# RWKV recurrence: one operand for state and outputs by tokens, head norm by tokens, inverse in two threads, exact overlaps and new prices in the emitter

## The chip, the cores and the metric

The kernel runs on one core of a Trainium2 chip. The metric is the device time of one execution in microseconds, lower is better. One core has five engines with a queue each: PE (matmuls), DVE and POOL (elementwise work), ACT (functions and copies) and SP, which here issues nearly all DMAs. Each engine works through its instructions in the order in which the program gives them.

## The reference, cut to what matters

One layer of a streaming encoder on 512 prompt tokens and 32 sample tokens: a joint input projection, three recurrent branches (SSD, GLA, RWKV-7), gates, output projection, cross attention. The change is in the RWKV branch:

```
S_new = S * w_t - (S @ kk_t) (kk_t * a_t)^T + v_t k_t^T        # per token, 16 heads of 64 x 64
o_t   = S_new @ r_t
o_rwkv = (head_layernorm(o7, ln_w, ln_b) + bonus) * silu(rgate)
```

The kernel computes it in chunks of 64 tokens: eight chunks for the prompt and one, number 8, for the sample. In a chunk the delta rule needs the inverse of a 64x64 triangular matrix per head.

## The kernel before, in words

A Python emitter writes out the whole program once (class `Sched`). It keeps a clock for each engine and a price for each operation, and runs generator threads in order of priority: a thread yields the time at which its next operand will be ready, and in the meantime the next thread emits. Prices decide only the order of the instructions; the chip then runs that order, with semaphores. The thread of lowest priority, `dense()`, emits the projections: 48 matmuls `pd` (272 columns, type f32r) for each block of weights, each block loaded (`wraw`), split by ACT into `wh` and by DVE into `wl`.

Of the blocks, 16 of 24 matmuls (memory keys and values), 2 and 24 (r, k, v) feed phase 1, the RWKV branch. 48 further blocks are fill (gates), emitted where nothing else is ready; the last 8 of them are held until late in phase 2 (`HOLD2`). So 384 + 26 x 48 + 40 x 48 = 3,552 dense matmuls can be emitted before phase 2 (SSD and GLA, `P2a`) opens, which `main()` does when all RWKV threads are done; phase 2 brings 28 blocks of its own.

RWKV runs by pairs of heads p = 0 to 7, in four threads: `rw_A` (decays, the products PP, tokens TK), `rw_I` (the inverse: 31 small steps on POOL, then matmuls pW, pT), `rw_C` (the recurrence over chunks 8, 0 to 7) and `rw_N` (head norm, bonus, store of y). A chunk of `rw_C` is a chain: matmul of the state (`pc<-Sn,AR`), DVE sum R, matmul `pc<-R,TT`, DVE predicated copy, matmul for the new state (`pc<-TK`), DVE update Sn. The outputs come from `pc<-AR,Sd` and `pc<-PP,TK`. Chunk 0 has no state, so it lacks the first and one of the others. `Sched.mm` prices an f32 matmul with a weight of more than 64 columns at 210 ns or more; f32 matmuls run as two passes, each with a weight load (PEld). `rw_N` sums over heads with f32r matmuls against a block matrix (`pl`, `pv`).

Of the kernel before, what the change touches and what calls it, by code (L numbers as in the profile page):

```python
# [8 lines left out]
F32 = mybir.dt.float32  # L9
# [93 lines left out]
class Pool:  # L103
# [5 lines left out]
    def tile(self, shape, dtype, name, tag=None, bufs=None):  # L109
        ring = self.rings.setdefault(tag or name, [])  # L110
        n = bufs or self.bufs
        if len(ring) >= n:
            self.S.flush(ring[-n])
        t = self.pool.tile(shape, dtype, name=name, tag=tag or name, **(dict(bufs=bufs) if bufs else {}))
        if len(ring) >= n:
            last = {}
            for v in self.S.reg.get(ring[-n], {}).values():
                for x in v:
                    for e, u in x.items():
                        last[e] = max(last.get(e, 0.0), u)  # L120
            self.S.reg[t.name] = {(0, 1 << 30, 0, 128): ({}, last)}
        ring.append(t.name)
        return t


class Sched:
# [57 lines left out]
    def span(self, a):  # L184
        x = a.ap
        if a.space == DRAM:
            return (a.offset, a.offset + sum((n - 1) * abs(s) for s, n in x) + 1, 0, 1)
# [4 lines left out]
        return (lo, lo + sum((n - 1) * s for s, n in x[1:]) + 1, p0, p0 + x[0][1])  # L192

    def since(self, a, which, e="pe"):
# [4 lines left out]
        lo, hi, p0, p1 = self.span(a)  # L199
        return max((t + (HOP.get((x, e), 0.0) if x != e or not which else 0.0) for k, v in d.items() if k[0] < hi and lo < k[1] and k[2] < p1 and p0 < k[3]  # L200
# [25 lines left out]
    def mm(self, out, lhsT, rhs, start, stop, transpose=False, shared=False):  # L226
# [102 lines left out]
def body(tc, I, O):  # L329
# [19 lines left out]
    with tc.manual_schedule(), \  # L349
# [242 lines left out]

        def start_mem():
# [36 lines left out]
            sq = slot[0]["TK"].rearrange("p a c h t -> p (a c h t)")[:, :8 * ML].rearrange("p (a t) -> p a t", t=ML)  # L630
# [12 lines left out]
        def start_x():  # L643
            xt = []
            for q, (b, a_) in enumerate(((slot[0]["AR"], 0), (slot[0]["PP"], 0), (slot[0]["PP"], 1), (slot[1]["AR"], 0))):
                yield has(f"load wk{q + W['XL']}")
                b = b if len(b.shape) == 4 else b.rearrange("p c h a t -> p c (h a) t")
                b = b.rearrange("p c a t -> p (c a t)")[:, a_ * 2 * T:(a_ + 1) * 2 * T].rearrange("p (a t) -> p a t", t=T)
# [8 lines left out]
            sq = slot[1]["TK"].rearrange("p a c h t -> p (a c h t)")[:, :T]  # L657
# [190 lines left out]
        def rw_A(p):  # L848
# [87 lines left out]

# [10 lines left out]
            S.tt(ar[:, :, 2, :], ch(rs), EE[:, :, 1:65], MUL)  # L947
            yield S.free("v")
# [15 lines left out]
            tk = d["TK"]  # L964

            def tokens(n_, src):
# [17 lines left out]
            pp = d["PP"]  # L984
            yield S.at(bk, ar)
            for c0, cn in ((0, 4), (4, 4), (8, 1)):
# [3 lines left out]
                for c in range(cn):  # L990
                    for i in range(2):
                        hs = slice(64 * i, 64 * i + 64)
                        S.mm(ps[i][:, c * 128:c * 128 + 128], bk[hs, c0 + c, i:i + 2, :].rearrange("p a t -> p (a t)"),
                             ar[hs, c0 + c, i:3:2 - i], True, True)
                for i in range(2):
                    S.tt(pp[:, c0:c0 + cn, i].rearrange("p c a t -> p c (a t)"), ps[i][:, :cn * 128].rearrange("p (c x) -> p c x", c=cn),
                         C("m_rw").unsqueeze(1).to_broadcast([128, cn, 128]), MUL)
                yield S.free("v")
            for i in range(2):
                S.store(out=rows64(n_scr[p % 2], i), in_=pp[i * 64:i * 64 + 64, :, i, 0, :])  # L1000
# [16 lines left out]
            for n_, (src) in enumerate((vs, kae, bee)):  # L1017
                S.mm(ps[0:64, n_ * 128:n_ * 128 + 128], src[:, 512:576], C("ident"), True, True, transpose=True)
            t8 = rwr.tile([64, 3, 128], F32, name="t8", tag="t8")
            yield S.since(t8, 1) - S.t["pe"]  # L1020
            S.act(t8.rearrange("p c t -> p (c t)"), ps[0:64, :384], AF.Copy)
            for i in range(2):
                h = 64 * i
                S.store(out=tk[64 - h:128 - h, :, 8, i, :], in_=t8[:, 0:2, h:h + 64])
                S.store(out=tk[h:h + 64, 1, 8, i, :], in_=t8[:, 2, h:h + 64])
            done.add(f"rwA{p}")

        def rw_I(p):

# [13 lines left out]
            S.dma(out=td, in_=I["eye3"])  # L1043
            yield has(f"rwN{p}")
            d = slot[p % NSLOT]
            pp, tt_ = d["PP"], d["TT"]
            yield S.stored(pp)
            for g in range(3):
                S.dma(out=nd[g * NB:g * NB + NB], in_=blocks(n_scr[p % 2]))
            yield S.at(nd, td)  # L1050
# [10 lines left out]
            yield S.stored(td)  # L1061
            for h in range(2):
                S.dma(out=tt_[h * 64:h * 64 + 64, :, h * 64:h * 64 + 64], in_=rows64(d_scr, h))
            yield S.at(tt_)
            x1 = rwr.tile([128, 8, 32], F32, name="x1", tag="itmp")
# [29 lines left out]
        def rw_C(p):  # L1095
# [6 lines left out]
            AR, PP, TK, TTt, GC = (d[n_] for n_ in ("AR", "PP", "TK", "TT", "GC"))  # L1102
            VU, KB = TK[:, 0], TK[:, 1]
            st_ = None
            yield S.stored(TK)
            yield S.at(s0r, PP, TK, TTt)
            RV = rwp.tile([128, 9, 64], F32, name="RV", tag="RV")
            for c0, cn in ((4, 5), (0, 4)):
                ps = yield from bank("pr")
                for c in range(cn):  # L1110
                    for i in range(2):
                        hs, gs = slice(64 * i, 64 * i + 64), slice(64 - 64 * i, 128 - 64 * i)
                        S.mm(ps[hs, c * 64:c * 64 + 64], PP[gs, c0 + c, i, 0, :], VU[gs, c0 + c, i, :], True, True)
                S.act(RV[:, c0:c0 + cn].rearrange("p c t -> p (c t)"), ps[:, :cn * 64], AF.Copy)
            for c in [8] + list(range(8)):
# [5 lines left out]
                pu, pS, po = pa[:, 128:256], pa[:, 256:384], pb[:, 0:128]  # L1121
                if Ss is None:
                    R = RV[:, 0]
                else:
                    S.mm(pa[:, 0:64], AR[:, c, 0:2, :].rearrange("p a t -> p (a t)"), Ss, True, True)
                    R = rwp.tile([128, 64], F32, name="R", tag="R", bufs=2)
                    S.tt(R, pa[:, 0:64], RV[:, c], ADD)
# [4 lines left out]
                nc.vector.copy_predicated(VU[:, c], two(C("blk1").bitcast(I32)), two(pu))  # L1132
                S.note("v", 203, (VU[:, c],), (pu,))
                yield max(S.at(VU[:, c]), 0.0 if Ss is None else S.at(Sd))
                S.mm(pS, KB[:, c].rearrange("p a t -> p (a t)"), VU[:, c], True, True)
                if Ss is not None:
                    S.mm(po, Sd.rearrange("p a t -> p (a t)"), both(AR[:, c, 2, :]), True, False)
                S.mm(po, VU[:, c].rearrange("p a t -> p (a t)"), PP[:, c, :, 1, :], Ss is None, True)
                ns = rwp.tile([128, 64], F32, name="Sn", tag="S", bufs=2)
                for i in range(2):  # L1140
                    hs = slice(64 * i, 64 * i + 64)
                    if Ss is None:
                        S.cp(ns[hs], pS[hs, hs])
                    else:
                        S.stt(ns[hs], Ss[hs], GC[hs, c, :], pS[hs, hs], MUL, ADD)
# [4 lines left out]
                for i in range(2):  # L1150
                    hs = slice(64 * i, 64 * i + 64)
                    S.act(AR[hs, c, 2, :], po[hs, hs], AF.Copy)
            done.add(f"rwC{p}")

        def rw_N(p):
# [3 lines left out]
            d = slot[p % NSLOT]  # L1159
            AR = d["AR"]  # L1160
            o7 = AR[:, :, 2, :]
            HC = ((0, 4, 0), (4, 4, 256), (8, 1, 512))

            def rows(t, c, n, o):
                w = min(64 * n, T - o)
                return t[:, o:o + w].rearrange("p (c t) -> p c t", c=n), o7[:, c:c + n, :w // n]

            oh = rwr.tile([128, T], F32R, name="oh", tag="hi")
            ol = rwr.tile([128, T], F32R, name="ol", tag="lo")
            cs = rwr.tile([128, T], F32, name="cs", tag="cs")  # L1170
            sq = rwr.tile([128, T], F32, name="sq2", tag="sq2")
            yield S.at(o7)
            for x in HC:
                h_, a_ = rows(oh, *x)
                parts(a_, h_, rows(ol, *x)[0])
            yield S.at(ol)
            for g, (o, w) in enumerate(((0, 256), (256, 288))):
                ps = yield from bank("pl")
                head_sums(ps[:, :w], oh[:, o:o + w], ol[:, o:o + w])
                for x in ((HC[0],), HC[1:])[g]:  # L1180
                    c_, a_ = rows(cs, *x)
                    S.stt(c_, rows(ps, x[0], x[1], 0)[0] if x[0] < 8 else ps[:, 256:288].unsqueeze(1), -1.0 / 64, a_, MUL, ADD)
                S.act(sq[:, o:o + w], cs[:, o:o + w], AF.Square)
            done.add(f"rwO{p}")
            sh = rwr.tile([128, T], F32R, name="sh", tag="hi")
            sl = rwr.tile([128, T], F32R, name="sl", tag="lo")
            parts(sq, sh, sl)
            yield S.at(sl)
            for (o, w) in HV:
                ps = yield from bank("pv")  # L1190
                head_sums(ps[:, :w], sh[:, o:o + w], sl[:, o:o + w])
                S.act(sq[:, o:o + w], ps[:, :w], AF.Ln, scale=1.0 / 64, bias=LNEPSC)
# [878 lines left out]
```

## Time and profile before

| | |
|---|---|
| median of 3 runs | 1308.95 us (1308.35 to 1311.31) |
| profiled execution | 1308.11 us, span 1306.3 us |
| PE busy | 1268.2 us, 97%, 10752 matmul passes |
| PEld (weight loads) busy | 1225.1 us, 94% |
| DVE, ACT, POOL busy | 840.3, 641.2, 368.2 us |
| chain that ended last | PE 61%, of which pd 47% |

Busy shares are averages: PE's records overlap, so that a matmul's price is read from the starts of its neighbours, not from its duration.

### The profile page before, as it was taken

Reading aid. Unit: us, or ns where it says so; the run is one execution under the profiler, and the core shown is the slowest. Engines: PE = TensorE matmul, PEld = TensorE weight load, DVE = VectorE, ACT = ScalarE, POOL = GpSimd, SP = SyncE. Lnnn points to the kernel's source line nnn. Section 1 sums busy time; section 2 is a strip of 40 time slices with the busy share of each in tenths; the row PEclk is TensorE's granted clock in tenths of the full one; section 3 lists DMA queues with packets and bytes.
Section 4 is the critical chain, followed back from the end, with each engine's and each line's share of the span. In section 5 each row is a group of like instructions: output and inputs, shape, how many; then the busy total and the mean of one; then the engine's idle time right before and its main releaser. Section 6 shows DMA issues by size and latency. Waiting matters only on the chain.

```text
span 1306.3 us, 27334 instructions
## 1 busy us (share of the span) xinstructions
PE 1268.2 (97%) x10752; PEld 1225.1 (94%) x10752; DVE 840.3 (64%) x1723; ACT 641.2 (49%) x1230; POOL 368.2 (28%) x724
## 2 busy tenths in 40 slices
PE   8899999999999999999999999998999999999996
PEld 7899989999999998999999999997999999999996
DVE  5747748767686777444455787576666756566543
ACT  5664554665557473553646455353545323544421
POOL 0712837464474736340101323032100000000000
PEclk8999999999999999999999999998999999999998
DMA  8543454453545354542532333243788345540201
GB/s 290 161 145 97 139 140 102 122 145 97 134 123 144 89 142 124 156 135 90 172 115 73 111 103 119 85 117 88 260 325 275 131 134 189 171 154 20 103 18 69
DMA packets 167696, 176.59 MB, mean 135 GB/s; under 512 B 99841, under 2 KB 122465, under 8 KB 167441
## 3 DMA queue, kind: packets, MB, share of 16 engines
q1 hardware_dynamic: 167136, 174.19, 43.7%
q8 instruction: 85, 1.39, 0.5%
q10 hardware_dynamic: 432, 0.67, 0.2%
q14 instruction: 43, 0.34, 0.1%
HBM read 134.01 MB, written 33.16 MB: 128 GB/s over the span
## 4 chain that ended last, share of the span: by engine, by line
PE 61%; DVE 4%; ACT 1%; issue 0%; DMA 0%; DVEq 0%; SPq 0%; ACTq 0%
PE pd L234 47%; PE pc L234 3%; PE pO L234 1%; PE py L234 1%; PE psc L234 1%; PE pov L234 1%; PE ph L234 1%; PE pS L234 1%; PE pT L231 1%; PE pss L234 1%; DMA ab<-acs_d 0%; DVE wl L273 0%; PE pp L234 0%; DVE seg L288 0%; ACT uh L267 0%
## 5 line engine op out<-in xcount | busy, mean ns | idle before, releaser
L234 PE MATMUL pd<-ul,wh 128*128 128x272 f32 (+1 forms) x1632 | 436.7, 295 | 0.0
L234 PE MATMUL pd<-uh,wh 128*128 128x272 f32 (+1 forms) x1632 | 432.2, 294 | 2.0 <-ACT wh L267 2.0
L234 PEld LDWEIGHTS pd<-uh,wh 128*128 128x128 f32 (+1 forms) x1632 | 307.7, 189 | 5.2 <-ACT wh L267 2.6
L234 PEld LDWEIGHTS pd<-ul,wh 128*128 128x128 f32 (+1 forms) x1632 | 307.9, 189 | 3.6 <-issue 2.2
L234 PE MATMUL pd<-uh,wl 128*128 128x272 f32 (+1 forms) x1632 | 250.0, 291 | 0.3 <-DVE wl L273 0.3
L234 PEld LDWEIGHTS pd<-uh,wl 128*128 128x128 f32 (+1 forms) x1632 | 219.8, 188 | 3.2 <-issue 1.2
L273 DVE TENSOR_TENSOR wl<-wraw,wh 128x1024 fp32r<-128x1024 f32 (+1 forms) x143 | 184.2, 1290 | 45.8 <-ACT wh L267 44.5
L267 ACT ACTIVATE wh<-wraw 128x1024 fp32r<-128x1024 f32 (+1 forms) x143 | 149.6, 1047 | 66.1 <-PE pd L234 36.0
L234 PE MATMUL pd<-uh,wr 128*128 128x256 f32 (+1 forms) x768 | 148.5, 291 | 0.0
L273 POOL TENSOR_TENSOR im<-td,nd 108x84 f32<-108x84 f32 (+23 forms) x248 | 100.6, 405 | 80.3 <-ACT sq L267 24.2
L234 PEld LDWEIGHTS pd<-uh,wr 128*128 128x128 f32 x768 | 121.0, 188 | 0.8 <-issue 0.4
L273 POOL TENSOR_TENSOR macc<-macc,hrs 128x288 f32<-128x288 f32 x3 | 3.0, 1026 | 372.3 <-ACT hrs L267 372.3
L273 POOL TENSOR_TENSOR td<-td,im 108x84 f32<-108x84 f32 (+23 forms) x248 | 102.2, 412 | 19.4
L234 PE MATMUL pd<-ul,wr 128*128 128x256 f32 (+1 forms) x384 | 99.8, 291 | 0.0
L234 PEld LDWEIGHTS pd<-ul,wr 128*128 128x128 f32 x384 | 72.4, 189 | 1.6 <-issue 1.2
L267 ACT ACT_TABLE_LOAD x55 | 70.6, 1283 | 2.2 <-DVE tB L273 1.3
L267 ACT ACTIVATE AR<-pc 64x64 f32<-64x64 f32 x144 | 31.0, 215 | 48.0 <-PE pc L234 47.2
L267 ACT ACTIVATE lerpA<-pd,par 128x272 f32<-128x272 f32 x50 | 24.4, 488 | 58.9 <-PE pd L234 52.4
L282 DVE SCALAR_TENSOR_TENSOR fg<-fg,pd 128x272 f32<-128x272 f32 x48 | 20.7, 433 | 44.5 <-ACT fg L267 43.4
L294 POOL COPY convo<-xp 128x3 f32<-128x3 f32 x24 | 7.7, 351 | 144.9 <-ACT xp L267 144.9
L267 ACT ACTIVATE fg<-pd,dpar 128x272 f32<-128x272 f32 x48 | 23.3, 485 | 44.7 <-PE pd L234 38.6
L282 DVE SCALAR_TENSOR_TENSOR Sn<-Sn,GC,pc 64x64 f32<-64x64 f32 x112 | 31.2, 279 | 20.9 <-PE pc L234 19.9
(483 smaller groups left out, 2572.7 us busy)
## 6 DMA issues: line engine op xcount, KB each, us to landing
wraw<-in_wall SPq DMA_DIRECT2D x165, 512.0 KB
g_mg<-fg SPq DMA_DIRECT2D x24, 272.0 KB
mgt<-g_mg SPq DMA_DIRECT2D x24, 272.0 KB
TK<-tm SPq DMA_DIRECT2D x96, 64.0 KB
ab<-acs_d SPq DMA_DIRECT2D x8, 512.0 KB
nd<-n_scr SPq DMA_DIRECT2D x24, 144.0 KB
n_scr<-PP SPq DMA_DIRECT2D x16, 144.0 KB
TT<-d_scr SPq DMA_DIRECT2D x16, 144.0 KB
```

The lines of the kernel that those rows point to most:

```text
L231: self.nc.tensor.transpose(out, lhsT, rhs)
L234: self.nc.tensor.matmul(out, lhsT, rhs, start=start, stop=stop, skip_group_check=shared)
L267: self.nc.scalar.activation(out=out, in_=in_, func=f, scale=scale, bias=bias)
L273: eng.tensor_tensor(out=out, in0=a, in1=b, op=op)
L282: self.nc.vector.scalar_tensor_tensor(out=out, in0=a, scalar=s, in1=b, op0=op0, op1=op1)
L294: (self.nc.vector if e == "v" else self.nc.gpsimd).tensor_copy(out=out, in_=a)
```

## The change

It does the following. (1) New state and outputs of a chunk come from one weight: tile NK holds PP and TK side by side, `NK[:, c, i, 1:3]` has the 64 columns of key tokens and the 64 of the outputs' product, and two matmuls of 64 columns give both; the state's part of the outputs is a second 64-column matmul `px` beside the first; `pc<-R,TT` has 64 columns instead of the same 64 twice; Sd goes. (2) Outputs lie by tokens, and `rw_N` sums over a head's 64 columns on DVE (TENSOR_REDUCE), then turns the result with 18 matmuls of 64x64 (`pl<-con,cs`) and applies weight and bias in ACT's copy. (3) `rw_I` ends after the POOL steps, and the rest is a thread of its own, `rw_J`. (4) The emitter compares overlaps by a bit mask of columns, not by first and last column. (5) It prices an f32 matmul of a wide weight at 107 ns or more, no longer 210, and a transpose of at most 64 rows at 40.

```diff
-            self.S.reg[t.name] = {(0, 1 << 30, 0, 128): ({}, last)}
+            self.S.reg[t.name] = {(0, 1 << 30, 0, 128, 0): ({}, last)}
...
-            ns = 107.0
+            ns = 107.0 if k > 64 else 40.0
...
-                ns = max(210.0, n * 1.67)
+                ns = max(107.0, n * 1.67)
...
-            d = dict(AR=pool.tile([128, 9, 3, 64], F32, name=f"AR{i}"))
-            d["PP"] = pool.tile([128, 9, 2, 2, 64], F32, name=f"PP{i}")
+            d = dict(AR=pool.tile([128, 9, 4, 64], F32, name=f"AR{i}"))
+            d["NK"] = pool.tile([128, 9, 2, 4, 64], F32, name=f"NK{i}")
-            d["TK"] = pool.tile([128, 2, 9, 2, 64], F32, name=f"TK{i}")
...
+            done.add(f"rwJ{p}")
+        def rw_J(p):
+            yield has(f"rwJ{p}")
...
-                pu, pS, po = pa[:, 128:256], pa[:, 256:384], pb[:, 0:128]
+                pu, px = pa[:, 64:128], pb[:, 128:192]
+                VU, R = NK[:, c, :, 3, :], NK[:, c, 0, 0, :]
...
+                    S.mm(px, AR[:, c, 2:4, :].rearrange("p a t -> p (a t)"), Ss, True, True)
-                    Sd = rwp.tile([128, 2, 64], F32, name="Sd", tag="Sd", bufs=2)
-                    S.tt(Sd, both(Ss), two(C("blk1")), MUL)
...
-                S.mm(pu, TTt[:, c, :], both(R), True, True)
+                S.mm(pu, TTt[:, c, :], R, True, True)
...
-                S.mm(pS, KB[:, c].rearrange("p a t -> p (a t)"), VU[:, c], True, True)
-                if Ss is not None:
-                    S.mm(po, Sd.rearrange("p a t -> p (a t)"), both(AR[:, c, 2, :]), True, False)
-                S.mm(po, VU[:, c].rearrange("p a t -> p (a t)"), PP[:, c, :, 1, :], Ss is None, True)
+                for i in range(2):
+                    S.mm(pb[:, i * 64:i * 64 + 64], NK[:, c, i, 1:3, :].rearrange("p a t -> p (a t)"), VU[:, i, :], True, True)
...
+            S.tt(x[:, 1:9], x[:, 1:9], NK[:, 1:9, 1, 3, :], ADD)
+            S.stt(cs, sums("mean", x).to_broadcast([128, 9, 64]), -1.0 / 64, x, MUL, ADD)
...
+            S.act(sq, cs, AF.Square)
+            va = sums("var", sq)
+            S.act(va, va, AF.Ln, scale=1.0 / 64, bias=LNEPSC)
+            S.act(va, va, AF.Exp, scale=-0.5)
...
+            S.tt(cs, cs, va.to_broadcast([128, 9, 64]), MUL)
...
+                        S.mm(ps[hs, c * 64:c * 64 + 64], cs[gs, c0 + c, :], C("ident")[gs, gs], True, True)
+                S.act(y[:, c0 * 64:c0 * 64 + w], ps[:, :w], AF.Identity, scale=Pm("ln_w", p), bias=Pm("ln_b", p))
+            S.tt(y, y, bo, ADD, e="p")
+            S.store(out=y_scr["rwkv"][p], in_=y)
...
-        S.add(rw_all(rw_I, "rwI_end"), 1)
+        S.add(rw_all(rw_J, "rwI_end"), 1)
+        S.add(rw_all(rw_I), 1)
```

How the order of the instructions moves is seen at three places. First PE at the end of the RWKV branch. Before, the last norm of pair 7 (`pv`) stands between dense blocks (`pd`):

```order
L234 MATMUL pd_8508<-uh_78,wl_8408 128x272 x4
L234 MATMUL pv_8529<-sh_8495,blk1_96 128x272
L234 MATMUL pv_8529<-sl_8496,blk1_96 128x272
L234 MATMUL pv_8533<-sh_8495,blk1_96 128x272
L234 MATMUL pv_8533<-sl_8496,blk1_96 128x272
L234 MATMUL pd_8508<-uh_78,wl_8408 128x272 x4
L234 MATMUL pd_8549<-uh_78,wh_8407 128x272
```

3,332 dense matmuls stand ahead of those `pv`, and 148 more between them and phase 2's first matmul, `pgk`. With the change, PE has this in place of it, from the middle of chunk 6 of pair 7 to the first matmuls of phase 2:

```order
L245 MATMUL pc_8676<-R_8680,TT1_124 128x64
L245 MATMUL pc_8677<-NK1_123 128x64 x2
L245 MATMUL pc_8692<-Sn_8686,AR1_122 128x64
L245 MATMUL pc_8693<-Sn_8686,AR1_122 128x64
L245 MATMUL pc_8692<-R_8696,TT1_124 128x64
L245 MATMUL pc_8693<-NK1_123 128x64 x2
L245 MATMUL pl_8724<-con_69,cs_8710 64x64 x8
L245 MATMUL pl_8734<-con_69,cs_8710 64x64 x10
L245 MATMUL pgk_8810<-smt_132,gw2_8776 128x272
L245 MATMUL pgk_8814<-smt_132,gw2_8776 128x272
L245 MATMUL pd_8821<-uh_78,wh_8798 128x272
```

All 3,552 dense matmuls stand ahead of chunk 5 of that pair, so that chunks 5, 6 and 7, the norm's `pl` and `pgk` follow one another with no dense matmul between them.

Second, one chunk of the recurrence on PE. Before, its last three matmuls have 128 columns each:

```order
L234 MATMUL pc<-TK_126 128x128
L234 MATMUL pc<-AR_123,Sd 128x128
L234 MATMUL pc<-PP_124,TK_126 128x128
```

With the change a chunk has these, dense matmuls between the three rows left out:

```order
L245 MATMUL pc<-Sn,AR_122 128x64 x2
...
L245 MATMUL pc<-R,TT_124 128x64
...
L245 MATMUL pc<-NK_123 128x64 x2
```

A chunk with a state has five matmuls before and five now, chunk 0 three and three; the columns of four and of three of them fall from 128 to 64.

Third, SP with the change, from the last store of RWKV's y to the first weights of phase 2 (`wraw`):

```order
L327 DMA y_rwkv<-yr 128x544
L327 DMA out_shift<-sho 128x50
L327 DMA m_ssd<-in_con 128x128
L327 DMA gw_8776<-in_gw 16x512
L327 DMA g_8778<-in_s_gla 128x1024
L327 DMA s_8780<-in_con 128x576
L327 DMA wraw<-in_wall 128x1024 x2
```

That is the order of before but for one store and one small load; what moved is the place of `wraw` against the dense work that PE still has, of which none is left.

## Rows read from the trace of the kernel before

**Rows 1.** Busy time by stretch (from:to, length, then each engine, clock, DMA).

```profile
94.00:630.00 536.00, 524.54 (x4846) 506.72 (x4845) 359.83 (x835) 286.99 (x597) 262.57 (x579) 1.00 0.46 122
630.00:660.00 30.00, 29.93 (x237) 29.05 (x236) 17.05 (x25) 21.64 (x33) 3.83 (x7) 1.00 0.57 188
```

**Rows 2.** PE's waits from 94 to 630 us: total, times, longest.

```profile
PE pc L234 <- DVE R L273: 3.0, 5, 1.6
PE pc L234 <- DVE TK L1132: 2.3, 4, 0.9
```

**Rows 3.** Timeline of PE in pair 7: start, us, what.

```profile
615.34 0.39 PE L234 MATMUL pc<-AR,Sd 128*128 128x128 f32 x2
615.56 0.39 PE L234 MATMUL pc<-PP,TK 128*128 128x128 f32 x2
...
616.29 0.29 PE L234 MATMUL pd<-ul,wh 128*128 128x272 f32 x1
616.42 0.33 PE L234 MATMUL pc<-Sn,AR 128*128 128x64 f32 x2
616.56 0.37 PE L234 MATMUL pd<-uh,wh 128*128 128x272 f32 x1
616.77 0.29 PE L234 MATMUL pd<-ul,wh 128*128 128x272 f32 x1
616.89 0.29 PE L234 MATMUL pd<-uh,wh 128*128 128x272 f32 x1
```

**Rows 4.** Timeline of the weight loads around 32-column matmuls of the attention.

```profile
1230.40 0.53 PEld L234 LDWEIGHTS pov<-pts,vs 128*128 128x128 f32 x4
1230.85 0.30 PEld L234 LDWEIGHTS pov<-pT,vh 128*128 128x128 f32 x2
```

**Rows 5.** Timeline of PE around 18 matmuls of 64x64.

```profile
473.72 1.26 PE L234 MATMUL pr<-TK,PP 64*64 64x64 f32 x36
474.96 0.41 PE L234 MATMUL pc<-s0r,AR 128*128 128x64 f32 x2
```

**Rows 6.** Timeline of all engines in one chunk, its chain's steps.

```profile
346.79 0.23 DVE L273 TENSOR_TENSOR R<-pc,RV 128x64 f32<-128x64 f32 x1
...
347.07 0.49 PE L234 MATMUL pc<-R,TT 128*128 128x128 f32 x2
...
347.87 0.30 DVE L1132 COPY_PREDICATED TK<-con,pc 128x128 f32<-128x128 int32 x1
...
348.22 0.49 PE L234 MATMUL pc<-TK 128*128 128x128 f32 x2
...
348.74 0.57 DVE L282 SCALAR_TENSOR_TENSOR Sn<-Sn,GC,pc 64x64 f32<-64x64 f32 x2 [0.58 <-PE pc L234]
```

**Rows 7.** Timelines of ACT, DVE, POOL after pair 7's last chunk.

```profile
629.94 1.28 ACT L267 ACT_TABLE_LOAD   x1
...
640.05 1.05 ACT L267 ACTIVATE wh<-wraw 128x1024 fp32r<-128x1024 f32 x1
...
649.24 1.05 ACT L267 ACTIVATE wh<-wraw 128x1024 fp32r<-128x1024 f32 x1
...
635.09 0.72 DVE L273 TENSOR_TENSOR cs<-cs,sq 128x544 f32<-128x544 f32 x1
...
637.70 1.36 POOL L273 TENSOR_TENSOR cs<-cs,bo 128x544 f32<-128x544 f32 x1
641.49 0.53 POOL L1226 MEMSET AT<- 128x512 f32 x1 [2.43 <-DMA y_rwkv<-cs]
```

**Rows 8.** Timeline of SP's queue in the same stretch.

```profile
636.97 0.33 SPq L316 DMA_DIRECT2D wraw<-in_wall  x1
639.09 0.32 SPq L316 DMA_DIRECT2D y_rwkv<-cs  x1
...
643.87 0.90 SPq L316 DMA_DIRECT2D wraw<-in_wall  x2
```

**Rows 9.** Busy time by stretch around one stop of PE.

```profile
183.00:192.00 9.00, 7.10 (x81) 6.44 (x77) 2.71 (x4) 4.95 (x9) 0.00 (x0) 0.81 0.74 214
```

More of the change, by code (lines that the diff above doesn't have):

```diff
@@ L133, in __init__ @@
         self.reg = {}
+        self.masks = {}
         self.banks = {}
@@ L186, in span @@
         if a.space == DRAM:
-            return (a.offset, a.offset + sum((n - 1) * abs(s) for s, n in x) + 1, 0, 1)
+            return (a.offset, a.offset + sum((n - 1) * abs(s) for s, n in x) + 1, 0, 1, 0)
         row = x[0][0]
@@ L191, in span @@
         p0 = p0() if callable(p0) else p0
-        return (lo, lo + sum((n - 1) * s for s, n in x[1:]) + 1, p0, p0 + x[0][1])
+        k = (lo, *((s, n) for s, n in x[1:]))
+        m = self.masks.get(k)
+        if m is None:
+            m = 1 << lo
+            for s, n in x[1:]:
+                if s:
+                    one, m = m, 0
+                    for i in range(n):
+                        m |= one << (s * i)
+            self.masks[k] = m
+        return (lo, lo + sum((n - 1) * s for s, n in x[1:]) + 1, p0, p0 + x[0][1], m)
     def since(self, a, which, e="pe"):
@@ L198, in since @@
             return 0.0
-        lo, hi, p0, p1 = self.span(a)
-        return max((t + (HOP.get((x, e), 0.0) if x != e or not which else 0.0) for k, v in d.items() if k[0] < hi and lo < k[1] and k[2] < p1 and p0 < k[3]
+        lo, hi, p0, p1, m = self.span(a)
+        return max((t + (HOP.get((x, e), 0.0) if x != e or not which else 0.0) for k, v in d.items() if k[0] < hi and lo < k[1] and k[2] < p1 and p0 < k[3] and (not k[4] or not m or k[4] & m)
                     for x, t in v[which].items()), default=0.0)
@@ L591, in body, with flat @@
         rsx = sp_.tile([128, T], F32, name="rsx")
+        def flat(a):
+            return a.rearrange("p c a t -> p (c a t)" if len(a.shape) == 4 else "p c h a t -> p (c h a t)")
         def start_mem():
@@ L946, in rw_A @@
             yield S.at(rs)
-            S.tt(ar[:, :, 2, :], ch(rs), EE[:, :, 1:65], MUL)
-            yield S.free("v")
+            for i in range(2):
+                hs = slice(64 * i, 64 * i + 64)
+                S.tt(ar[hs, :, 3 - i, :], ch(rs)[hs], EE[hs, :, 1:65], MUL)
+                yield S.free("v")
             bee = sq
@@ L963, in rw_A @@
             rwr = pools["rwR"][1]
-            tk = d["TK"]
+            nk = d["NK"]
             def tokens(n_, src):
@@ L978, in tokens @@
                     for r in range(2):
-                        S.store(out=tk[g:g + 64, min(n_, 1), r:8:2, i, :], in_=tm[r * 64:r * 64 + 64, :, h:h + 64])
+                        S.store(out=nk[g:g + 64, r:8:2, i, 1 + i if n_ else 3, :], in_=tm[r * 64:r * 64 + 64, :, h:h + 64])
                 yield S.free("a")
             yield from tokens(0, vs)
-            pp = d["PP"]
             yield S.at(bk, ar)
@@ L1016, in rw_A @@
             ps = yield from bank("ptk")
-            for n_, (src) in enumerate((vs, kae, bee)):
+            for n_, (src) in enumerate((kae, vs, bee)):
                 S.mm(ps[0:64, n_ * 128:n_ * 128 + 128], src[:, 512:576], C("ident"), True, True, transpose=True)
-            t8 = rwr.tile([64, 3, 128], F32, name="t8", tag="t8")
+            t8 = rwr.tile([64, 3, 128], F32, name="t8", tag="tm", bufs=TMB)
             yield S.since(t8, 1) - S.t["pe"]
@@ L1023, in rw_A @@
                 h = 64 * i
-                S.store(out=tk[64 - h:128 - h, :, 8, i, :], in_=t8[:, 0:2, h:h + 64])
-                S.store(out=tk[h:h + 64, 1, 8, i, :], in_=t8[:, 2, h:h + 64])
+                S.store(out=nk[64 - h:128 - h, 8, i, 1 + i:4:2 - i, :], in_=t8[:, 0:2, h:h + 64])
+                S.store(out=nk[h:h + 64, 8, i, 1 + i, :], in_=t8[:, 2, h:h + 64])
             done.add(f"rwA{p}")
@@ L1042, in rw_I @@
             tmp = rwr.tile([3 * NB, 96], F32, name="im", tag="itmp")
-            S.dma(out=td, in_=I["eye3"])
             yield has(f"rwN{p}")
-            d = slot[p % NSLOT]
-            pp, tt_ = d["PP"], d["TT"]
-            yield S.stored(pp)
+            yield S.stored(slot[p % NSLOT]["NK"])
+            yield max(0.0, S.since(nd, 1) - S.t["pe"])
             for g in range(3):
                 S.dma(out=nd[g * NB:g * NB + NB], in_=blocks(n_scr[p % 2]))
+            yield max(0.0, S.since(td, 1) - S.t["pe"])
+            S.dma(out=td, in_=I["eye3"])
             yield S.at(nd, td)
@@ L1064, in rw_I @@
             yield S.at(tt_)
-            x1 = rwr.tile([128, 8, 32], F32, name="x1", tag="itmp")
+            x1 = rwr.tile([128, 8, 32], F32, name="x1", tag="xw")
             for h in (0, 64):
@@ L1101, in rw_C @@
             yield has(f"rwI{p}")
-            AR, PP, TK, TTt, GC = (d[n_] for n_ in ("AR", "PP", "TK", "TT", "GC"))
-            VU, KB = TK[:, 0], TK[:, 1]
+            AR, NK, TTt, GC = (d[n_] for n_ in ("AR", "NK", "TT", "GC"))
             st_ = None
-            yield S.stored(TK)
-            yield S.at(s0r, PP, TK, TTt)
-            RV = rwp.tile([128, 9, 64], F32, name="RV", tag="RV")
+            yield S.stored(NK)
+            yield S.at(s0r, NK, TTt)
             for c0, cn in ((4, 5), (0, 4)):
@@ L1158, in rw_N @@
             rwr = pools["rwR"][1]
[L1159 to L1183, printed above, removed]
@@ L1184, in rw_N @@
-            done.add(f"rwO{p}")
[L1185 to L1192, printed above, removed]
+            NK = slot[p % NSLOT]["NK"]
+            x = NK[:, :, 0, 3, :]
@@ new lines, in rw_N, with sums @@
+            yield S.at(x)
+            def sums(name, a):
+                t = rwr.tile([128, 9, 1], F32, name=name, tag=name)
+                nc.vector.tensor_reduce(out=t, in_=a, op=ADD, axis=AX.X)
+                S.note("v", 680, (t,), (a,))
+                return t
+            S.tt(x[:, 1:9], x[:, 1:9], NK[:, 1:9, 1, 3, :], ADD)
+            yield S.free("v")
+            cs = rwr.tile([128, 9, 64], F32, name="cs", tag="cs")
+            sq = rwr.tile([128, 9, 64], F32, name="sq2", tag="hi")
@@ L1193, in rw_N @@
+            S.stt(cs, sums("mean", x).to_broadcast([128, 9, 64]), -1.0 / 64, x, MUL, ADD)
+            done.add(f"rwO{p}")
+            yield S.at(cs)
+            S.act(sq, cs, AF.Square)
+            yield S.at(sq)
+            va = sums("var", sq)
+            S.act(va, va, AF.Ln, scale=1.0 / 64, bias=LNEPSC)
+            S.act(va, va, AF.Exp, scale=-0.5)
             bo = rwr.tile([128, T], F32, name="bo", tag="hi")
             S.dma(out=bo, in_=b_scr[p])
-            S.act(sq, sq, AF.Exp, scale=-0.5)
@@ L1196, in rw_N @@
-            yield S.at(sq, bo)
-            S.tt(cs, cs, sq, MUL)
-            S.ts(cs, cs, Pm("ln_w", p), MUL, Pm("ln_b", p), ADD, e="p")
-            S.tt(cs, cs, bo, ADD, e="p")
-            S.store(out=y_scr["rwkv"][p], in_=cs)
+            yield S.at(va)
+            S.tt(cs, cs, va.to_broadcast([128, 9, 64]), MUL)
+            yield S.at(cs)
+            y = rwr.tile([128, T], F32, name="yr", tag="yr")
+            for c0, cn, w in ((0, 4, 256), (4, 5, 288)):
+                ps = yield from bank("pl")
+                for c in range(cn):
+                    for i in range(2):
+                        hs, gs = slice(64 * i, 64 * i + 64), slice(64 - 64 * i, 128 - 64 * i)
+                        S.mm(ps[hs, c * 64:c * 64 + 64], cs[gs, c0 + c, :], C("ident")[gs, gs], True, True)
+                S.act(y[:, c0 * 64:c0 * 64 + w], ps[:, :w], AF.Identity, scale=Pm("ln_w", p), bias=Pm("ln_b", p))
```

60 lines of the change are left out of this document (32 added, 28 removed).

## The prediction

> **What bounds the kernel now.** I read the busy time by stretch first: in the RWKV phase, 94 to 630 us, PE is busy for 524.5 of 536 us, and in the 30 us after it without a gap [rows 1]. So PE is the bound, and a change is worth what it takes from PE's work or from PE's stops. The stops are few: PE's list of waits shows 3.0 us for the sum R and 2.3 for the predicated copy as the largest in this phase [rows 2], 11.5 us in all as the difference of the two numbers of the stretch. Next I read what a matmul costs PE, from starts in the timeline. Dense matmuls follow each other at 0.12 us (616.77 to 616.89), and a 128-column f32 matmul starts 0.22 us after its like (615.34 to 615.56) [rows 3].
>
> **PE's work in the recurrence: 0 us.** The change halves the columns of four of the five matmuls of a chunk and leaves their number (chunk 0: three of three). So the question is the price of 64 columns. One such matmul exists before, `pc<-Sn,AR`: from the dense start ahead of it (616.29) to the second behind it (616.77) is 0.48 us, less two dense ones of 0.125 leaves 0.23 [rows 3], no less than the 128-column one. The reason shows where matmuls of 32 columns follow one another: four weight loads of 128 columns take 0.45 us (1230.40 to 1230.85), 0.11 each [rows 4]; an f32 matmul is two passes with a load each, so 0.22 us is its floor whatever its columns. 64 + 8 chunks keep 5 x 64 + 3 x 8 = 344 matmuls at 0.22. The other bound is the floor of half the columns, 0.11 each, 38 us less in all; I take 0, since `pc<-Sn,AR` is the same shape.
> The Trainium skill (TensorE: Matmul & The Clock Gate, Back-to-back issue gap) lists about 60 cycles for a matmul of up to 64 columns and 134 for 128, by which the 38 us would be gained and the sum below would be about 1302. Its section LDWEIGHTS makes a load's time a matter of weight columns alone, 107 ns at 128, by which nothing is gained; the trace agrees with this one, 0.11 us a load.
>
> **PE's work in the norm: +3 us.** Out go eight f32r matmuls of 256 to 288 columns a pair, 8 x 0.125 = 1.0 us at the dense rate. In come 18 of 64x64, the shape and count of `pr`: 1.24 us (473.72 to 474.96) [rows 5], and about 0.1 for changing over. 8 x 0.35 = 3.
>
> **What the new price does to the order: the end of phase 1.** The emitter now believes 107 ns where the chip takes 220. Its PE clock runs 344 x 0.1 = 35 us short over phase 1, and it fills the time that it believes free with 35 / 0.125 = 280 more dense matmuls; the order shows it (3,332 ahead of the last norm before, all 3,552 now). Then the fill is at an end, since what is left is held or belongs to phase 2. Before, the 148 dense matmuls after `pv` and more behind them covered the norm's tail, the store and phase 2's first loads (PE 29.9 of 30 us [rows 1]). Now chunks 5, 6, 7, the norm of pair 7 and the change of phase lie open on PE. All of it is one chain, which I add up:
>
> Chunks: a matmul's two passes to DVE's next step 0.52 (348.22 to 348.74); R and hand-over 0.28; `pc<-R,TT` to the copy 0.80; copy and hand-over 0.35; two key matmuls to the update 0.52, update 0.57 [rows 6], hand-over about 0.1. That is 3.1 us; PE works 5 x 0.22 = 1.1 of it, so 2.0 idle, three times: 6.0.
>
> Norm: three small copies of ACT, 0.85 by the size of the update pair; five DVE steps of 512 to 576 columns (sum, two reductions, centre, scale) of some 0.75, by the 0.72 of one of 544 [rows 7]: 3.7; a square on ACT 0.7; two table loads of 1.28 [rows 7], of which the first runs under a reduction: 1.75; Ln and Exp of nine columns 0.4; nine hand-overs of 0.05 [rows 6] to 0.25, I take 0.15: 1.3. Together 8.7 (7.8 to 9.6 by the hand-overs).
>
> Tail: ACT's copy out of PSUM 0.7 and hand-over 0.2; POOL's sum 1.36 [rows 7]; the store of y from 639.09 until POOL, which waited for its landing, goes on at 641.49: 2.4; from there to the issue of `wraw` at 643.87, behind four loads on SP: 2.4 [rows 7, 8]; landing 3.1 (issue at 636.97, split at 640.05) to 5.4 (643.87 to 649.24) [rows 7, 8], I take 4.3, as half a megabyte and more lies ahead of it on the same queues; split by ACT 1.05 and hand-over 0.2. That is 12.6, less 0.5 of work of `pgk`: 12.1.
>
> PE's stop is 6.0 + 8.7 + 12.1 = 27 us (24 to 31).
>
> Clock: after a PE stop of 1.6 us at about 185 us the granted clock of that stretch is 0.81 [rows 9], that is, part of it went at 1.2 and not 2.4 GHz; 19% of 9 us is 1.7 us. Over a longer stop with slow matmuls in it I take 2 us (1 to 5).
>
> **What comes back: -6 us.** Up to this point PE is later than the emitter thinks, by some 4 us a pair, and the other engines are not. So PE will less often reach a chain's step too early. Of the 11.5 us of stops I take half (0 to 11.5).
>
> **What costs nothing.** The inverse in two threads lets POOL begin the next pair earlier; POOL is busy for 263 of 536 us [rows 1], and PE waits for it hardly at all, so its 31 steps stay under dense work. Sd leaves DVE, px adds a copy on ACT; both engines have over 170 us free in the phase [rows 1], and their steps lie beside PE's 40 us of dense work a pair. The exact masks touch only the order. If that cover ends, as for chunks 5 to 7, the copies count, and they are in the sum. Past the change of phase, the order is nearly that of before; the dense work is the same in total.
>
> **Sum**, against the profiled execution's own 1308.1 us (0.85 below the median shown): 0 + 3 + 27 + 2 - 6 = +26, so 1334.
>
> **The rivals.**
> (A) A 64-column pass costs its columns, 0.11 us a matmul: 38 us come out of PE, the emitter's price is right, PE is not late and the 6 us don't come back: 1308 + 3 + 27 + 2 - 38 = 1302, faster. Against it stand [rows 3, 4]; for it, that the two passes of `pc<-Sn,AR` might be slow only for standing alone between dense matmuls. It decides from a price under 0.22 - 32 / 344 = 0.13 us. 10%.
> (B) New waits in phase 1: one tile NK takes the writes of DMA, DVE and ACT that went to three, and SP's queue, in which the weights stand behind stores, is written for a PE that is faster than the real one. 0.3 us a chunk, 22 us in all, instead of the 6 that come back: 1362. The low price of waits so far [rows 2] speaks against it. 6%.
> (C) The open end is shorter, as landing and hand-overs are at their low ends (24), and all stops go (-11.5): 1308 + 3 + 24 + 1 - 11.5 = 1325. 14%.
> (D) The change does nothing: the branch ends under cover anyway, because what DVE, ACT and SP do there is ready long before PE. But the norm needs PE's last chunk, and the store and the loads need the norm, so only a tail of loads could go. 1306 to 1310. 3%.
>
> **How the numbers follow.** My case, 1334 with its own bounds 1327 to 1344 (1308 + 3 + 24 + 1 - 9 to 1308 + 3 + 30 + 4 - 1: the terms' ends, short of all of them at once), holds 67%. Reaching down over (C) to 1318 and up to 1346 leaves out (A), (B) and (D), and some of the edges. Under 0.2%, 2.6 us, a measurement of this kernel can't tell a change from none: slower are my case, (B), (C), 87%; the same (D), 3%; faster (A), 10%.
>
> **What the profile after would show.** Starts of 64-column matmuls 0.22 us apart in a row of them, or 0.11 if (A) holds. One stop of PE of some 27 us at about 655 us, in pieces: chunks, the norm, then one piece of about 12 us that ends with `wh<-wraw`. The granted clock low there. PE's waits for R and the copy in phase 1 at half. The prediction is wrong if PE in phase 1 waits longer than before, or if the dense work resumes before the store of y has landed.

## The result and the profile after

The changed kernel takes 1341.86 us (median of 4 runs, 1341.04 to 1346.47) against 1309.65 us before on the same chip: 1.0243 times, 95% interval 1.0225 to 1.0262. The profiled execution has 1341.04 us and a span of 1339.1, 32.8 more than before.

The page after, first PE's busy line, then PE and its granted clock in the 40 slices (33.5 us each):

```profile
span 1339.1 us, 27735 instructions
...
PE 1278.3 (95%) x10976; PEld 1233.7 (92%) x10976; DVE 825.6 (62%) x1643; ACT 635.3 (47%) x1260; POOL 381.5 (28%) x716
...
PE   8899999999999999999669999998999999999997
...
PEclk8999999999999999999769999998999999999999
```

Two slices in the middle, 636 to 703 us, have lost a third of PE, and the clock falls with them. The rest is as full as before. Busy time by stretch (length, then each engine with its instructions, then the clock) shows the place:

```profile
94.00:649.20 555.20, 545.62 (x5223) 529.31 (x5222) 349.76 (x751) 285.89 (x624) 271.64 (x572) 0.99 0.46 124
649.20:683.00 33.80, 11.42 (x74) 9.01 (x73) 7.32 (x18) 8.92 (x22) 2.13 (x6) 0.57 0.26 86
683.00:692.00 9.00, 8.08 (x37) 7.76 (x36) 6.56 (x9) 6.15 (x10) 0.00 (x0) 0.52 0.35 112
692.00:705.00 13.00, 11.57 (x96) 11.17 (x95) 5.76 (x7) 6.54 (x11) 0.00 (x0) 1.00 0.10 28
```

Up to 649.2 us PE stops for 9.6 us in all (555.2 less 545.6; it was 11.5 in the stretch of [rows 1]). Then it has work for a third of 34 us, where before it had 29.9 us in 30 [rows 1]. The timeline of PE there (start, us, what, idle before it and who ended that):

```profile
658.16 1.11 PE L245 MATMUL pc<-NK 128*128 128x64 f32 x4 [0.39 <-DVE NK L1150]
667.69 2.19 PE L245 MATMUL pl<-con,cs 64*64 64x64 f32 x36 [8.41 <-DVE cs L284]
676.32 2.15 PE L245 MATMUL pgk<-smt,gw 16*128 16x272 f32 x4 [6.45 <-DMA gw<-in_gw]
682.50 0.59 PE L245 MATMUL pd<-uh,wh 128*128 128x272 f32 x1 [4.03 <-ACT wh L278]
...
691.20 0.43 PE L245 MATMUL pd<-uh,wh 128*128 128x272 f32 x1
691.43 0.36 PE L245 MATMUL pd<-ul,wh 128*128 128x272 f32 x1
691.63 0.28 PE L245 MATMUL pd<-uh,wh 128*128 128x272 f32 x1
691.75 0.29 PE L245 MATMUL pd<-ul,wh 128*128 128x272 f32 x1
```

The last dense block before the stop ends at 649.2, the next begins at 682.50: chunks 5 to 7 lie open until 659.3, then the norm (8.41), then store, loads and split. Dense matmuls then start 0.23 us apart up to 691.43, and 0.12 from 691.63 on. At 687.4 and 701.8 PE stops twice more for weights that are late:

```profile
687.41 2.18 PE L245 MATMUL pd<-uh,wl 128*128 128x272 f32 x8 [0.92 <-DVE wl L284]
...
701.83 0.39 PE L245 MATMUL pd<-uh,wh 128*128 128x272 f32 x1 [1.43 <-ACT wh L278]
```

What stands in the last piece is seen in the timelines of SP, POOL and ACT:

```profile
671.99 0.32 SPq L327 DMA_DIRECT2D y_rwkv<-yr  x1
674.41 0.52 POOL L1240 MEMSET AT<- 128x512 f32 x1 [2.45 <-issue]
675.53 0.92 SPq L327 DMA_DIRECT2D wraw<-in_wall  x2
681.39 1.06 ACT L278 ACTIVATE wh<-wraw 128x1024 fp32r<-128x1024 f32 x1 [10.88 <-DMA wraw<-in_wall]
```

The store of y, the wait for its landing, the weights behind it on SP and their split are the steps that lay under dense work before [rows 7, 8].

### The profile page after: what moved, and what is told of

It reads as the page before. It is cut to its first block, busy times and chain, and to the rows that moved or that the text cites. A ratio compares the mean times of both kernels' runs of the same rounds, so it can differ in the third digit from the quotient of the medians.

```text
span 1339.1 us, 27735 instructions
## 1 busy us (share of the span) xinstructions
PE 1278.3 (95%) x10976; PEld 1233.7 (92%) x10976; DVE 825.6 (62%) x1643; ACT 635.3 (47%) x1260; POOL 381.5 (28%) x716
## 5 line engine op out<-in xcount | busy, mean ns | idle before, releaser
L284 DVE TENSOR_TENSOR wl<-wraw,wh 128x1024 fp32r<-128x1024 f32 (+1 forms) x143 | 179.7, 1260 | 32.5 <-ACT wh L278 32.1
L284 POOL TENSOR_TENSOR im<-td,nd 108x84 f32<-108x84 f32 (+23 forms) x248 | 111.3, 449 | 195.0 <-DMA td<-in_eye 86.8
L284 POOL TENSOR_TENSOR td<-td,im 108x84 f32<-108x84 f32 (+23 forms) x248 | 104.9, 423 | 19.4
L278 ACT ACTIVATE fg<-pd 128x272 f32<-128x272 f32 x48 | 18.8, 395 | 81.5 <-PE pd L245 70.1
L293 DVE SCALAR_TENSOR_TENSOR fg<-fg,pd 128x272 f32<-128x272 f32 x48 | 20.9, 437 | 56.3 <-ACT fg L278 55.9
L278 ACT ACTIVATE NK<-pc 64x64 f32<-64x64 f32 (+1 forms) x208 | 38.3, 214 | 30.7 <-DVE Sn L293 27.9
```

What stands on the lines that cost most here:

```text
L278: self.nc.scalar.activation(out=out, in_=in_, func=f, scale=scale, bias=bias)
L284: eng.tensor_tensor(out=out, in0=a, in1=b, op=op)
L293: self.nc.vector.scalar_tensor_tensor(out=out, in0=a, scalar=s, in1=b, op0=op0, op1=op1)
```

## The experiments

Theory 1 is that of the prediction: the emitter's price opens the end of phase 1, and 64 columns cost what 128 do. Against it stand theory 2, that the new structure itself costs, and theory 3, that 64 columns are cheaper.

**64 columns against 128 (wide128).** The five matmuls of a chunk get 128 columns again; one of them for example:

```diff
-                S.mm(pu, TTt[:, c, :], R, True, True)
+                S.mm(pu, TTt[:, c, :], both(R), True, True, cols=64)
```

> The changed kernel, in which the five matmuls of a chunk have 128 columns again: each repeats its 64 columns, and the second half is never read. The emitter still takes 107 ns for them, so the order of all engines is that of the changed kernel. Theory 1 and 2 (a pass costs its weight load, not its columns, up to 128): no change, 1338 to 1346 us, and two matmuls between dense ones take 0.447 us as with 64 columns. Theory 3 (64 columns are cheaper): 344 matmuls by up to 0.11 us, up to 38 us more, 1380.

Measured: 1344.33 us (1342.75 to 1346.02), 1.0253 (1.0237 to 1.0268), beside 1.0243 for the changed kernel. The same place of pair 7 in the two timelines of PE, first the changed kernel, then wide128:

```profile
646.64 0.29 PE L245 MATMUL pd<-ul,wh 128*128 128x272 f32 x1
646.76 0.33 PE L245 MATMUL pc<-R,TT 128*128 128x64 f32 x2
646.90 0.37 PE L245 MATMUL pd<-uh,wh 128*128 128x272 f32 x1
647.11 0.29 PE L245 MATMUL pd<-ul,wh 128*128 128x272 f32 x1
```

```profile
641.60 0.29 PE L245 MATMUL pd<-ul,wh 128*128 128x272 f32 x1
641.72 0.38 PE L245 MATMUL pc<-R,TT 128*128 128x128 f32 x2
641.86 0.37 PE L245 MATMUL pd<-uh,wh 128*128 128x272 f32 x1
642.07 0.29 PE L245 MATMUL pd<-ul,wh 128*128 128x272 f32 x1
```

Durations differ, the starts don't: 0.47 us from the dense matmul ahead to the second behind, in both. Less two dense ones (0.125 each) that is 0.22 for a matmul of either width. Theory 3 falls.

**The price alone (before107).** The kernel before, in which only the emitter's number for the chunk's five matmuls changes:

```diff
-                ns = max(210.0, n * 1.67)
+                ns = max(107.0 if cols else 210.0, n * 1.67)
```

> The kernel before, in which the emitter prices the five matmuls of a chunk at 107 ns; nothing else is changed, and the matmuls keep their 128 columns. Theory 1: the fill ends before chunk 5 of pair 7, as in the changed kernel; chunks, old norm and tail lie open on PE for some 28 us, low clock and late weights add 7, some 6 to 8 come back in phase 1: 1333 to 1342 us. Theory 2 (the structure costs, not the price): 1306 to 1313.

Measured: 1333.63 us (1331.1 to 1334.2), 1.0167 (1.0152 to 1.0182). All matmuls, copies and DMAs are those of before. PE's timeline shows the end open, as in the changed kernel:

```profile
644.41 0.41 PE L234 MATMUL pc<-R,TT 128*128 128x128 f32 x2
...
673.47 2.15 PE L234 MATMUL pgk<-smt,gw 16*128 16x272 f32 x4 [9.98 <-DMA gw<-in_gw]
680.16 0.59 PE L234 MATMUL pd<-uh,wh 128*128 128x272 f32 x1 [4.54 <-ACT wh L267]
```

No dense matmul starts between 644.4 and 680.16. So the price of these five matmuls by itself costs 22 us, as theory 1 says, and up to there PE stops for less than in the kernel before (6.4 us from 94 to 643, where [rows 1] gives 11.5). The new price of small transposes was not tested apart.

**The true price (price223).** The changed kernel with the price that its trace shows (the edit gives it to wider f32 matmuls after phase 1 too, whose price was 427 ns for 256 columns):

```diff
-                ns = max(107.0, n * 1.67)
+                ns = 223.0
```

> The changed kernel, with one number set otherwise: the emitter's price of an f32 matmul of a wide weight is 223 ns, what the trace of the changed kernel shows (0.447 us for two such matmuls of 64 columns between dense ones), no longer 107. Theory 1 (the price put the fill too early, and the end of phase 1 lies open): 3,279 dense matmuls stand ahead of the last chunk again, the stop of 33 us at 649 us is gone, and so are the low clock and the late weights behind it; what stays is the norm's 2.7 us on PE: 1312 us (1308 to 1317). Theory 2 (the new structure costs: one tile NK with more waits, the longer norm): the loss stays for the most part, 1330 us or more. Theory 3 (64 columns are really cheaper, the price of 107 is right): 223 makes PE's order too sparse, but the work saved is there: under 1300.

Measured: 1334.05 us (1332.62 to 1337.44), 1.0178 (1.0159 to 1.0196). The end of phase 1 is covered now, and PE is full behind it, but phase 1 has got worse (busy time by stretch):

```profile
94.00:656.00 562.00, 541.12 (x5112) 519.83 (x5112) 356.73 (x761) 288.27 (x636) 279.95 (x575) 0.98 0.43 119
656.00:700.00 44.00, 43.97 (x358) 43.03 (x355) 19.36 (x28) 23.62 (x37) 2.16 (x6) 1.00 0.45 155
```

PE stops for 20.9 us up to 656, against 11.5 before and 9.6 in the changed kernel. Counted by work: 3,552 dense matmuls and all of RWKV are done at 681.5 us, and at 660.0 before, 21.5 later, of which 1.3 were there at 85 us and 2.7 are the norm's matmuls; some 17.5 were lost within phase 1. Of these, 9.4 are stops that the busy time shows (20.9 less 11.5). A further part is the granted clock, which falls in three places to its lower level (busy time by stretch):

```profile
168.00:174.50 6.50, 6.29 (x39) 5.65 (x39) 2.01 (x5) 1.43 (x2) 5.17 (x18) 0.50 0.14 28
263.50:266.50 3.00, 3.00 (x15) 3.00 (x15) 1.02 (x3) 2.74 (x5) 2.08 (x7) 0.50 0.80 231
373.00:379.00 6.00, 6.00 (x57) 5.78 (x56) 1.23 (x4) 2.29 (x8) 0.08 (x1) 0.50 0.85 178
```

That is over 15 us at 0.50, where the kernel before has some 3 in this phase [rows 9]. As dense matmuls start 0.23 us apart at this level and not 0.125, the difference costs some 6 us at most, by estimate; what is left is stops too short to show as idle time. So the end is covered, as theory 1 says, but the time is the one that theory 2 named: the change loses about as much by either half alone, and the two losses don't add (1.0167 and 1.0178, together 1.0243).

One such stop of price223 in its timelines of SP, DVE and PE:

```profile
364.08 1.29 SPq L327 DMA_DIRECT2D TT<-d_scr  x2
...
367.32 0.44 DVE L1089 STREAM_TRANSPOSE x<-TT 64x256 f32<-64x256 f32 x1 [2.38 <-DMA TT<-d_scr]
369.06 0.44 DVE L1089 STREAM_TRANSPOSE x<-TT 64x256 f32<-64x256 f32 x1 [1.31 <-DMA TT<-d_scr]
...
370.21 0.72 DVE L284 TENSOR_TENSOR r<-rs,r 128x544 fp32r<-128x544 f32 x1
...
370.98 0.39 PE L245 MATMUL pbn<-r,blk 128*128 128x272 f32 x1 [2.48 <-DVE r L284]
```

Two transposes of the inverse stand on DVE ahead of their loads. DVE stops for 3.7 us, and r, which PE needs for pbn and which needs none of it, is queued behind.

**Which part of the structure.** Four edits of the changed kernel, the first three at 223 ns. The copy t8 in another buffer (t8own):

```diff
-            t8 = rwr.tile([64, 3, 128], F32, name="t8", tag="tm", bufs=TMB)
+            t8 = rwr.tile([64, 3, 128], F32, name="t8", tag="yr")
```

> The changed kernel at the price of 223 ns, with one buffer moved: the copy t8 (tokens of chunk 8) no longer shares the two buffers tm with the copies of the other chunks but lies in that of the norm's result (yr). At 223 ns the trace shows 17.5 us more stops of PE in phase 1 than before, and ACT held five times (4.7 us, up to 2.3) at t8 until stores out of tm have landed, with what PE waits for queued behind it. Theory 4 (that shared buffer makes a good part of the stops): 1322 to 1329 us, and ACT's waits at t8 gone. Theory 5 (the stops are many small ones of the new structure: px ahead of R, POOL's earlier inverse, weights in one tile): 1331 to 1336.

Measured: 1337.71 us (1334.98 to 1339.23), 1.0209 (1.0189 to 1.023): no gain, and above both ranges. ACT's waits at t8 are gone, and PE now waits for the loads of the state s0r, which cost 0.9 us in price223 (PE's waits in phase 1: total, times, longest):

```profile
PE pc L245 <- DMA s0r<-in_s_rwkv: 9.7, 4, 5.8
```

The matmul px behind the one with R (px_late):

```diff
-                    S.mm(px, AR[:, c, 2:4, :].rearrange("p a t -> p (a t)"), Ss, True, True)
...
                 S.mm(pu, TTt[:, c, :], R, True, True)
+                if Ss is not None:
+                    S.mm(px, AR[:, c, 2:4, :].rearrange("p a t -> p (a t)"), Ss, True, True)
```

> The changed kernel at the price of 223 ns, with one matmul moved: px (the state's part of the outputs) follows the matmul with R and no longer stands ahead of it. Theory 5a (px delays R by 0.22 us in each of 64 chunks, so that PE or the order pays): up to 14 us come back, 1320 to 1328. Theory 4 or another cause: 1331 to 1336, as px is only work that stands there anyway.

Measured: 1344.45 us (1342.69 to 1350.18), 1.0271 (1.0241 to 1.03): slower than with px ahead of R, which neither theory expected.

The inverse in one thread (one223; rw_IJ runs rw_I, then rw_J):

```diff
-        S.add(rw_all(rw_J, "rwI_end"), 1)
-        S.add(rw_all(rw_I), 1)
+        S.add(rw_all(rw_IJ, "rwI_end"), 1)
```

> The changed kernel at the price of 223 ns, with the inverse in one thread again (the part after the POOL steps runs in the same thread, so the next pair's POOL steps begin only after it). Theory 5b (POOL's steps of the next pair, begun earlier, stand ahead of POOL's copies of the pair in work, for which PE waits: 1.7 us for bk at about 165 us): PE's waits for bk go, 1325 to 1331; but 3,552 dense matmuls stand ahead of phase 2's first matmul, so that some us may open there. Theory 4 or another cause: 1332 to 1340.

Measured: 1365.54 us (1364.28 to 1367.47), 1.0425 (1.0403 to 1.0447). By the ratios (1.0425 beside 1.0178) the joined thread costs 32 us more, the opposite of 5b and outside both ranges. Up to the end of phase 1 PE stops for 37.4 us (94 to 687), 16.5 more than in price223; another 7.0 us of stops stand behind it (698.6 to 730), where no dense matmul of phase 1 is left. PE's waits in phase 1 name what I had expected to go:

```profile
PE pp L245 <- POOL bk L305: 8.7, 5, 2.3
PE pc L245 <- DVE R L284: 8.1, 7, 2.6
PE pc L245 <- DVE NK L1150: 4.9, 5, 2.4
```

In the changed kernel and in price223 the first of them is 1.7 us, once. Why POOL's copy bk is late more often here was not tested.

Both moves of the first two at the price of 107 ns (px_t8_107):

> The changed kernel at its own price of 107 ns, with both moves (t8 out of the buffers tm, px behind the matmul with R). The emitter then puts 3,336 dense matmuls ahead of the last norm and 111 between it and phase 2's first, so that the end of phase 1 is covered although the price is half the true one. Theory 1 with 4 (the open end, and the waits of the shared buffer): both losses are gone, the 2.7 us of the norm stay and PE, behind the emitter's clock, waits less than before: 1303 to 1314. If the stops in phase 1 come from another part of the structure: 1318 to 1335.

Measured: 1319.21 us (1315.62 to 1322.99), 1.0072 (1.0049 to 1.0095). This is the best of the new structure, 1.7% under the changed kernel at the same price: the end is covered, and 3,552 dense matmuls with RWKV are done at 667.8 us, 7.8 after before. But its stops in phase 1 (94 to 638 us) are 18.6 us, the largest of them (5.5 us) a wait of PE for ACT's copy W. That is the second of the two expected cases: the two moves don't take away the waits of phase 1.

**More fill for the open end (hold0).** The changed kernel with `HOLD2=0` for 8.

> The changed kernel with its price of 107 ns, in which no block of fill is held for late in phase 2 (HOLD2 0 for 8): 384 more dense matmuls may go into phase 1, and 3,692 stand ahead of the last norm, 120 more between it and phase 2's first matmul. Theory 1: the stop of 33 us at the end of phase 1 is gone, which gives back some 35 us; late in phase 2 384 dense matmuls are missing, and stops open there of up to that size: 1308 to 1340, with the end of phase 1 covered in any case. Theory 2 (structure): PE still stops at the end of phase 1 or loses as much within it, 1335 or more.

Measured: 1343.39 us (1342.13 to 1347.52), 1.0242 (1.0225 to 1.0259), above the range of theory 1. Yet neither case of theory 2 came about: the end of phase 1 is covered (PE 39.95 of 40 us from 660 to 700), and the loss stands later in full, where phase 2 passes into the next:

```profile
972.47 1.34 PE L245 MATMUL ph<-xe,btok 128*128 128x512 f32 x2
998.62 0.82 PE L245 MATMUL pd<-o__12260,wh 128*128 128x272 f32 x2 [24.80 <-ACT wh L278]
```

So here the fill that phase 1 used was missing at the end of phase 2.

**Parts alone on the kernel before (bmask, bthreads, bmask_160, bmaskthreads_160).** The diffs are the change's own lines for the masks and for `rw_J` (with it a later load of `td` and a buffer of its own, `xw`); the last two have 160 ns for 210 as well.

> The kernel before, with the exact overlaps alone (bit masks in the emitter; price 210, all else as before). As many dense matmuls stand ahead of the last chunk as before (3,279) and between norm and phase 2. If the new loss of 17.5 us in phase 1 at the true price comes from the masks (steps believed ready that are not): 1318 to 1328. If it comes from the recurrence's and norm's new structure: no change, 1306 to 1314.

Measured: 1311.41 us, 1.0008 (0.9994 to 1.0022): the masks change nothing here.

> The kernel before, with the inverse in two threads alone (price 210, old overlaps). With the new structure, joining the two threads cost 31 us. If two threads help whatever the structure: they can take here no more than the some 26 us of stops that phase 1 has in all, 1295 to 1305. If they only repair what the new structure brings: no change, 1306 to 1315.

Measured: 1328.27 us (1325.59 to 1330.65), 1.013 (1.0107 to 1.0153): 17 us slower, outside of both expectations. The largest stop, in the timelines of SP, ACT and PE:

```profile
180.29 6.41 SPq L316 DMA_DIRECT2D TK<-tm  x8
186.79 2.49 SPq L316 DMA_DIRECT2D TK<-t  x4
...
190.02 0.37 SPq L316 DMA_DIRECT2D g_rwkv<-fg  x1
...
192.78 0.40 ACT L267 ACTIVATE fg<-pd 128x272 f32<-128x272 f32 x1 [13.19 <-DMA g_rwkv<-fg]
...
193.70 0.59 PE L234 MATMUL pd<-uh,wh 128*128 128x272 f32 x1 [6.01 <-DVE fg L282]
```

Twelve stores of tokens keep SP's queue for 8.9 us; the store of the fill's result fg stands behind them, ACT can't write the next fg until it has landed, PSUM isn't emptied, and PE stops for 6.0 us in its dense work.

> The kernel before, with the exact overlaps and a price of 160 ns for the five matmuls of a chunk. The emitter's PE clock is then some 20 us short over phase 1, yet 3,332 dense matmuls stand ahead of the last norm and 148 between it and phase 2, as before. Theory 1 (a low price costs only by the end that it opens, and gives back waits in phase 1 since PE lags): 1302 to 1309. If a low price loses by itself: 1313 or more.

Measured: 1310.8 us (12 runs), 0.9997 (0.9985 to 1.0008): between the two ranges. A price that is 50 ns lower costs nothing while the end stays covered, but gives nothing back either.

> The same with the inverse in two threads too; the counts at the end of phase 1 are again those of before (3,332 and 148). Theory 1: 1301 to 1309. If threads or masks bring waits of their own: 1312 or more.

Measured: 1317.18 us, 1.0055 (1.0035 to 1.0075): 6 us more than without the two threads (bmask_160), in a third order. No version beats the kernel before.

## Why the prediction was right, and where it was off

The time lies inside the range and inside the likeliest case's own bounds (1327 to 1344); by spans the sum is 32.8 us for the 26 predicted.

**The bound and the recurrence: held.** 64 columns cost 0.22 us as 128 do; wide128 shows it, and rival (A) is out. Of the two rules of the Trainium skill (TensorE: Matmul & The Clock Gate), the one in LDWEIGHTS, time by weight columns alone, agrees with the 0.22. The table in Back-to-back issue gap, which that section gives for an isolated matmul without the budget of a weight load, doesn't describe these f32 matmuls.

**The norm: held.** 18 matmuls of 64x64 stand in place of the eight; by the starts around them their cost is 1.34 us a pair, 2.7 in all for the 3 taken.

**The open end: held, and it is the main term.** Between 649.2 and 682.5 us lie 33.3 us; 15 + 18 matmuls and pgk would take 5.1 of them at full clock (15 x 0.22, 1.24, 0.5), so the stop is 28.2 for the 27 predicted. By pieces: chunks 10.1 us with their work (3 x 3.1 predicted), norm 8.4 (8.7), from the end of `pl` at 669.9 to the first dense matmul 12.6 (12.1 and 0.5 of work). Two errors cancelled in the last: the store and the queue took 3.5 us (671.99 to 675.53) and not 4.8, landing of `wraw` 5.9 (to 681.39) and not 4.3. That the price causes it is shown by before107, which changes nothing else and has a like stop.

**The clock: undersized.** Some 34 dense matmuls from 682.5 to 691.4 start 0.23 and not 0.125 us apart: 3.4 us for the 2 taken, within 1 to 5. **Late weights: missing.** Behind the stop PE waits twice more for new weights (0.9 and 1.4 us); I had none of it.

**What came back: in size only by difference.** At the 3,701st dense matmul the changed kernel is 29.9 us behind (708.4 for 678.5). The terms so far give 28.2 + 3.4 + 2.4 + 2.7 = 36.7 there, so 6.8 came back, for the 6 of a possible 11.5. This number is a remainder, and the prediction's reason, half of the stops, covers little of it: the stops that the trace shows fell from 11.5 to 9.6 only, and where the rest comes from stays open. PE's waits for R fell from 3.0 [rows 2] to 1.7 us, those for the predicated copy from 2.3 to none up to 649 us. That a PE that lags waits less is shown only in part: stops fell at 107 ns in both structures (11.5 to 6.4, and 20.9 to 9.6), and bmask_160 gained nothing.

**Later: missing.** Another 2.9 us come after 708 us, in small pieces, to 32.8. No run tests them.

**"What costs nothing": held in the sum, not in its reason.** It said that the two threads, px and the masks touch only work under cover. For the masks bmask bears it out. But at the true price the new structure loses some 17.5 us in phase 1, and the kernel before loses 17 us with the two threads alone (6 with masks and 160 ns). The changed kernel doesn't show this loss: it stops for 9.6 us in phase 1. The likely reason, argued and not shown, is that at 107 ns the emitter puts far more dense work between the steps of its threads, and this covers their waits, at the cost of the end. If so, the same price opens the end and hides the waits, and the zero of this term was right by luck. New waits like rival (B)'s are there at the true price and absent from the changed kernel; that they have the cause (B) names, the one tile NK, no run shows. Neither (C) nor (D) occurred.

Which part of the new structure makes its waits stays open; the tile NK, the new norm and the price of small transposes were never tested apart. t8own, px_late, one223 were each meant to take one wait away; the order moved with every edit, and by the ratios they came out 4, 12 and 32 us slower. With an emitter that re-plans everything, an edit is not an isolated step, and a difference of 10 us between two such orders can't be put down to the line that was edited. That holds for the two threads too: together they cost 17 us in one order and 6 in another, and in the new structure joining them cost 32.

## What to carry to other kernels

Where a planner fills the gaps of a chain with independent work, a price that is too low need not show in the stage that it is for, as here; look for it at the end, where the fill is used up and nothing covers the chain, the store and the next loads. Measure a matmul's price from the starts of its neighbours before halving its columns: here the weight load set it. And test a part alone on the old kernel as well as undone in the new one, since here two halves that cost 22 us each made 32 together.

## What the runs showed of the hardware

A store of tokens costs SP's queue 0.80 us apiece where eight stand together (6.41 us in bthreads), and a load of weights 0.46 (0.92 for two in the changed kernel): the queue's time doesn't go by bytes (64 KB a store, 512 KB a load), and what stands behind many small stores lands late.

The granted clock of the changed kernel is 1.00 from 649.2 to 654.0 us, in the first chunks of the open chain, and 0.50 from there to 691.5, through the rest of the chain and on for 9 us of dense work. It rose after PE had worked without a stop since 687.4. A stop of PE thus costs some us beyond its own length. Shorter stops do so too: in price223 the 2.48 us before 370.98 are followed by a stretch at 0.50 from 373 to 379.
